# Bank order at three stage changes, and a block's sums of exponentials ahead of the maxima of its slot

## The chip, the core and the metric

The kernel runs on one core of a Trainium2 chip. A core has TensorE (PE), VectorE (DVE), ScalarE (ACT), GpSimd (POOL) and SyncE (SP, which here only issues DMAs); they run their own instruction streams and wait for each other by semaphores. PSUM, where PE writes, has 8 banks of 2 KB for each of 128 partitions; PE, DVE and ACT reach it. The metric is the device time of one execution in microseconds (us): the median of the runs is compared, and one execution more was taken with the hardware profiler.

## The reference, cut to what matters

One step of a trunk of two layers on 128 context tokens and 1024 latent tokens, 1024 wide. Layer 0 has neighbourhood attention beside a state-space mixer, layer 1 grouped-query attention; each layer ends with a gated convolutional feed-forward net (2816 wide).

```python
def odd_mixer(h, od, ctx):              # 16 query heads, 4 key/value heads of 64
    hp = h @ w_in
    q, k, v = ...
    q = rope_2d(rmsnorm(q, q_g)); k = rope_2d(rmsnorm(k, k_g))
    o = blocked_attention(q, jnp.concatenate([k, k_ctx], axis=1), jnp.concatenate([v, v_ctx], axis=1))
    return o.reshape(B, L, GQA_HEADS * HEAD_DIM) @ w_out, None
...
s = jnp.einsum('bqkgd,btkd->bkgqt', qi, k) * scale
p = jax.nn.softmax(s, axis=-1)
o = jnp.einsum('bkgqt,btkd->bqkgd', p, v)
...
x = x + g1 * out                        # output projection, residual
x = x + g2 * conv_ffn(h, w_up, conv_w, conv_b, w_down)
```

## The kernel before

All large products are done in two parts: a weight or an activation is split into a high part (`w_hi`, `mixh`, a copy on ACT that rounds) and a low one (`w_lo`, `mixl`, a subtraction on POOL or DVE), and PE adds three products, hi x hi, hi x lo, lo x hi. Every weight tile so passes SP (load of `w_raw`), ACT (L888) and POOL (L74) before PE has it. There are 4 buffers of `w_raw` and 3 each of `w_hi` and `w_lo`.

**PSUM by stages.** Pools of banks are opened and closed as the stages change. Odd projection: psN1 (2 banks), then psP (3) and psW (3). Grouped attention: psM1 (4), psS1 (2), psO1 (2). Second output projection and feed-forward net: psN2 (1), psD (7). A new pool takes the banks in the order in which it is opened, so that order decides which bank waits for whose last reader.

**Grouped attention (`Grouped.run`, with `finish`, `maxima`, `queries`, `rest`).** t = 0 to 7 goes over pairs of query heads, c = 0, 1 over halves of 512 queries, kt = 0 to 8 over blocks of 128 keys; s = 9c + kt is the slot. In a slot PE makes two score tiles (`gq_ps`, L68) in psS, ACT takes the exponentials (L834), PE adds the slot before to `gq_po` with v (L818, psO), and POOL sums the exponentials into `gq_acc` (DVE at kt = 1). In the same slots PE prepares the maxima for t + 1: matmuls into banks of psM (L735, four in a slot, two in slots 4, 6, 9 and 12, the last by slot 14), each followed by a reduction on DVE (`gq_mx`, L737). psM has four banks in rotation, called `gq_m`; the matmuls that use them take them in the order of issue.

`finish` is a generator that brings the block before to its end while the next one runs. `run` calls `next(done)` once in each slot from kt = 2:

- kt = 2: the sums over keys, called pd: four matmuls of `gq_acc` with ones into a bank of psM (L764); ACT copies two rows out of it (`gq_dn`, L773); SP reshapes them by a load (`gq_d`).
- kt = 4: DVE takes the reciprocals (L780); SP stores them (`d_dn`) and loads them back spread over the partitions (`gq_rd`).
- kt = 7: DVE multiplies, `mix <- gq_po, gq_rd`.

In block (7, 1) the reciprocals (L768) are taken directly from pd's bank, in four pieces. In slot 6 the queries of t + 2 are loaded (`gq_q`, two loads of 576 KB), as soon as their buffer is free, on the same queue of SP as the loads above.

**Order.** In `run` the order of PE and DVE is as written (`manual_schedule`); ACT, POOL and SP, and all engines in the other stages, are ordered by a scheduler from what it takes for the durations, so an edit can move instructions in stages that it doesn't touch.

**Second output projection (`out_proj`).** `mix` is split into `mixh` and `mixl` in four chunks of tokens; then for c = 0, 1, for m = 0 to 7 (128 output features), for h = 0, 1 one accumulation of 24 matmuls (`ps_b`, 128 x 288), added to the residual x by DVE. The function serves both layers.

**Last down projection (L1366).** PE multiplies `ff_f`, which comes back from memory (`ff_r`), with weight tiles loaded one after the other on SP; the residual x is loaded there too.

Of the kernel before, what the change touches and what calls it, by code (L numbers as in the profile page):

```python
# [10 lines left out]
F32 = mybir.dt.float32  # L11
# [3 lines left out]
ALU = mybir.AluOpType  # L15
# [5 lines left out]
KT = 8  # L21
# [623 lines left out]
class Grouped:  # L645
# [104 lines left out]
    def run(self, mix, psM, psS, psO):  # L750
        K, S = self.K, self.S
# [7 lines left out]
        def finish(t, c, po, acc):  # L759

            qs = slice(512 * c, 512 * c + 512)
            pd = bank()
            for p in range(2):
                pe.matmul(pd[64 * p : 64 * p + 64], lhsT=K.ones[:, 0:64], rhs=acc[:, p], start=True, stop=True)  # L764
            rd = tp.tile([128, 512], F32, tag="rd", name="gq_rd", bufs=1)
            if (t, c) == (7, 1):
                for i in range(0, 512, 128):
                    dve.reciprocal(rd[:, i : i + 128], pd[:, i : i + 128])  # L768
                    K.tt(mix[:, t, qs][:, i : i + 128], po[:, i : i + 128], rd[:, i : i + 128], ALU.mult)
                return  # L770
            dn = tp.tile([65, 512], F32, tag="dn", name="gq_dn", bufs=1)
            for p in (0, 64):
                act.activation(dn[p : p + 1], pd[p : p + 1], AF.Copy)  # L773
            d8 = tp.tile([128, 8], F32, tag="d8", name="gq_d8", bufs=1)
            for p in range(2):
                K.load(d8[64 * p : 64 * p + 64], dn[64 * p : 64 * p + 1].rearrange("p (a b) -> p a b", b=8))
            yield
            yield
            r8 = tp.tile([128, 8], F32, tag="r8", name="gq_r8", bufs=1)
            dve.reciprocal(r8, d8)  # L780
            sd = S.dn[(2 * t + c) % 2]
            K.load(sd.rearrange("p (a b) -> (p a) b", b=8), r8)
            for p in range(2):
                K.load(rd[64 * p : 64 * p + 64], bass.AP(tensor=sd.tensor, offset=sd.offset + 512 * p, ap=[[0, 64], [1, 512]]))
            yield
            yield
            yield
            K.tt(mix[:, t, qs], po, rd, ALU.mult)
            yield
# [3 lines left out]
        with K.tc.manual_schedule(engines={mybir.EngineType.PE, mybir.EngineType.DVE}):  # L793
            for t in range(8):
                kv = t // 2
                kk, k2, qq, q2 = self.kk[kv], self.k2[kv], self.qq[t], self.q2[t]
                ahead = self.maxima(t + 1, tp, bank) if t < 7 else iter(())
                keys = self.keys(kv + 1) if t % 2 == 0 and t < 6 else iter(())
                leading = iter(())
                rest = self.rest(t + 1) if t < 7 else iter(())  # L800
                prompt = prompt_attention(
                    K,
                    tp,
                    bank,
                    bank,
                    [(self.qp[t][:, p], self.kp[kv], vt[:, 8, 64 * kv : 64 * kv + 64]) for p in range(2)],
                    mix[:, t, NL:],
                )
                for c in range(2):
                    qs = slice(512 * c, 512 * c + 512)  # L810
                    po = psO.tile([128, 512], F32, tag="o", name="gq_po")
                    acc = ep.tile([128, 2, 512], F32, tag="a", name="gq_acc")
                    pts = {}

                    def value(kt, pts=pts, po=po, acc=acc, kv=kv, t=t):
                        v = vt[:, kt if kt < 8 else 9, 64 * kv : 64 * kv + 64]
                        for p in range(2):
                            pe.matmul(po[64 * p : 64 * p + 64], lhsT=v, rhs=pts[kt][p], start=kt == 0, stop=kt == 8)  # L818
                        for p in range(2):
                            eng = dve if (p == 0 if t == 7 else kt == 1) else pool  # L820
                            if kt == 1:
                                K.tt(acc[:, p], pts[0][p], pts[1][p], ALU.add, eng)
                            elif kt > 1:
                                K.tt(acc[:, p], acc[:, p], pts[kt][p], ALU.add, eng)

                    for kt in range(9):
                        s = 9 * c + kt
                        ks = slice(128 * kt, 128 * kt + 128)
                        pts[kt] = []
                        for p in range(2):  # L830
                            ps = psS.tile([128, 512], F32, tag="s", name="gq_ps")
                            K.acc(ps, [(kk[:, ks], qq[:, p, qs]), (k2[:, ks], q2[:, p, qs])])
                            e = ep.tile([128, 512], F32, tag="p", name="gq_p", bufs=8)
                            act.activation(e, ps, AF.Exp, scale=0.125)  # L834
                            pts[kt].append(e)
                        if 1 <= s <= 5:
                            next(rest, None)
                        if s >= 5:
                            next(keys, None)
                        if s == 6 and t < 6:  # L840
                            self.queries(t + 2)
                            leading = self.leading(t + 2)
                        if s >= 13:
                            next(leading, None)
                        if s in (4, 6, 9, 12):
                            next(prompt, None)
                        while pend:
                            pend.pop(0)()
                        pend.append(lambda kt=kt, value=value: value(kt))
                        for _ in range(1 if s in (4, 6, 9, 12) else 2):  # L850
                            next(ahead, None)
                        if s == 15 and t < 7:
                            self.largest(t + 1)
                        if kt >= 2:
                            next(done, None)
                    for _ in done:
                        pass
                    done = finish(t, c, po, acc)
            while pend:
                pend.pop(0)()  # L860
            for _ in done:
                pass
# [520 lines left out]
def tile_hybrid_step(ctx, tc, I, O):  # L1383
# [204 lines left out]
    def out_proj(l, w, mp, mix, space, source):  # L1588
# [12 lines left out]
        gate = ada[l][:, 16:24]  # L1601
        feed = Feed(K, I, S, l, W, x, rs, A[l][1], ada[l][:, 24:32])
        beside = iter(())
        for c in range(2):
            for m in range(KT):
                cols = lambda ap: ap.rearrange("p (h c t) -> p c h t", h=2, c=2)[:, c]
                u = W.get(w[m])
                K.load(x[c][:, m], cols(source(m)))
                if c and m == KT - 1:
                    feed.tile(0)  # L1610
                for h in range(2):
                    a, b = QCH[2 * h + c]
                    ps = P("b")[:, :HW]
                    K.acc(ps, pairs(u, M(a, b), KT, colm))
                    for s0, s1, cd in segs(a, b):
                        xs = x[c][:, m, h, s0 - a : s1 - a]
                        K.stt(xs, ps[:, s0 - a : s1 - a], gate[:, m, cd : cd + 1], xs, ALU.mult, ALU.add)
                    at = (2 * c + h) * HW
                    norm.add(at, at + HW, x[c][:, m, h], m == KT - 1)
                    if m == KT - 1:  # L1620
                        with K.tc.high_priority():
                            norm.stats(at, at + HW, P)
                    for _ in range(2):
                        next(beside, None)
                    if c and m == KT - 1 and h == 0:
                        feed.ahead(1)
                K.load(cols(S.xs[:, m]), x[c][:, m])
            if c == 0:
                early.release()
                mp.release()  # L1630
                beside = feed.early()
                for _ in range(2):
                    next(beside)
# [87 lines left out]
                normed(u, q, m, a, b)  # L1721
    for p in (tp, norm, x_pool, PB):
        p.release()
    PB = K.psum("psP", b=3)
    psW = K.ps("psW")
    gq = Grouped(K, I, S)
    rp = K.sb("proj1o", 1, "right")
    for m, u, q in first[:2]:
# [31 lines left out]
    for p in (rp, np_, qp):  # L1760
        p.release()
    hp.release()
    psW.release()
    PB.release()
    PN.release()
    mp = K.sb("mix1")
    mix = mp.tile([128, 8, NT], F32, name="mix")
    psM, psS, psO = K.ps("psM1", 4), K.ps("psS1", 2), K.ps("psO1", 2)
    gq.room()
    gq.run(mix, psM, psS, psO)  # L1770
    for p in (psO, psS, psM):
        p.release()
    PN = K.psum("psN2", n=1)
    PB = K.psum("psD", b=7)
# [141 lines left out]
```

## Time and profile before

| | |
|---|---|
| median of 3 runs | 3207.27 us (3204.74 to 3210.99) |
| the profiled execution's own time | 3196.94 us |
| its span | 3195.1 us |
| mean granted clock of PE | 0.967 |
| busy: PE, DVE, ACT, POOL | 2958.6, 1845.8, 1401.5, 1100.6 us |
| grouped attention in the span | about 1840 to 2264 us |
| second output projection | about 2264 to 2379 us |
| last down projection | from about 2907 us to the end |

A row of the timeline gives the start, the duration, the engine, the line of the kernel, the operation with its output and inputs, the number of instructions, and in brackets the idle time before it with what ended that. The granted clock (PEclk) is 1.00 at 2.4 GHz and 0.50 at 1.2 GHz; a window with 0.66 had both.

### The profile page before, as it was taken

What the parts mean: (1) busy time and instruction counts of PE and PEld (TensorE: products, weight loads), DVE (VectorE), ACT (ScalarE), POOL (GpSimd) and SP (SyncE); (2) the same over time, 40 slices, a digit from 0 to 9 for tenths busy, and PEclk for the clock granted to TensorE, in tenths of its full rate; (3) what the DMA queues carried; (4) which work ended last, traced back from release to release, by engine and by line L of the source; (5) the groups of instructions that cost most, each with busy time, mean ns of one, the idle gap of its engine ahead of it and who ended that gap; (6) DMA issues with size and microseconds to landing.
All of it is one profiled execution on the core that took longest, in us unless ns stands there. A gap on an engine that the chain in (4) does not pass through costs nothing.

```text
span 3195.1 us, 49924 instructions
## 1 busy us (share of the span) xinstructions
PE 2958.6 (93%) x19218; PEld 2577.1 (81%) x19218; DVE 1845.8 (58%) x3570; ACT 1401.5 (44%) x2627; POOL 1100.6 (34%) x765
## 2 busy tenths in 40 slices
PE   4998869998999999899998999999888999999999
PEld 3996667797899999788888943434688999998999
DVE  8867856648665555342165666665486565654330
ACT  4335356646444444343253254445454434443332
POOL 1210221153111111355554466667631111113654
PEclk7999989999999999999999999999999999999999
DMA  6657573142212222776634411110331212126653
GB/s 231 167 188 230 172 171 66 32 139 74 69 63 83 75 71 83 255 256 223 227 112 122 119 44 43 26 41 11 122 97 49 83 63 83 63 83 212 209 190 106
DMA packets 207038, 379.56 MB, mean 119 GB/s; under 512 B 36304, under 2 KB 121552, under 8 KB 206672
## 3 DMA queue, kind: packets, MB, share of 16 engines
q1 hardware_dynamic: 206544, 376.31, 37.6%
q8 instruction: 151, 2.47, 0.3%
q14 instruction: 87, 0.71, 0.1%
q0 software_dynamic: 256, 0.07, 0.0%
HBM read 295.80 MB, written 75.13 MB: 116 GB/s over the span
## 4 chain that ended last, share of the span: by engine, by line
PE 46%; DVE 7%; DMA 3%; ACT 1%; issue 1%; SPq 0%; POOL 0%; DVEq 0%; ACTq 0%; POOLq 0%
PE ps_d L1366 16%; PE ps_u L1147 8%; PE ps_b L68 5%; PE ps_w L1147 4%; PE gq_ps L68 3%; PE gq_po L818 3%; PE ps_v L1147 2%; DVE gq_mx L737 2%; DMA w_raw<-in_w_down_dram 1%; DMA d_dn<-gq_r 1%; PE gq_m L735 1%; PE ps_n L933 1%; PE gq_m L764 1%; DVE x L74 1%; DMA gq_rd<-d_dn 1%
## 5 line engine op out<-in xcount | busy, mean ns | idle before, releaser
L74 POOL TENSOR_TENSOR w_lo<-w_raw,w_hi 128x1024 fp32r<-128x1024 f32 x194 | 484.0, 2498 | 579.3 <-ACT w_hi L888 550.7
L1366 PE MATMUL ps_d<-ff_f,w_hi 128*128 128x384 f32 x2112 | 551.8, 340 | 19.8 <-ACT w_hi L888 10.6
L1147 PE MATMUL ps_u<-q_T,ff_w 128*128 128x288 f32 x3168 | 448.3, 297 | 21.9 <-ACT ff_p L1161 15.9
L1147 PEld LDWEIGHTS ps_u<-q_T,ff_w 128*128 128x128 f32 x3168 | 432.0, 189 | 25.1 <-ACT ff_p L1161 17.7
L74 POOL TENSOR_TENSOR ff_w<-w_raw,ff_w 128x512 fp32r<-128x512 f32 x88 | 130.4, 1483 | 882.6 <-ACT ff_w L1135 882.6
L1366 PEld LDWEIGHTS ps_d<-ff_f,w_hi 128*128 128x128 f32 x2112 | 386.2, 190 | 47.6 <-issue 19.5
L1366 PE MATMUL ps_d<-ff_f,w_lo 128*128 128x384 f32 x1056 | 357.2, 338 | 1.5 <-POOL w_lo L74 1.5
L888 ACT ACTIVATE w_hi<-w_raw 128x1024 fp32r<-128x1024 f32 x194 | 204.5, 1055 | 326.3 <-PE ps_d L1366 157.1
L74 POOL TENSOR_TENSOR gq_acc<-gq_acc,gq_p 128x512 f32<-128x512 f32 x210 | 275.1, 1339 | 135.5 <-DVE gq_acc L74 94.4
L71 DVE SCALAR_TENSOR_TENSOR ff_g<-ff_G,pack,ff_g 128x127 f32<-128x127 f32 (+2 forms) x264 | 167.3, 647 | 197.6 <-ACT ff_g L1184 192.9
L1135 ACT ACTIVATE ff_w<-w_raw 128x512 fp32r<-128x512 f32 x266 | 165.4, 624 | 199.6 <-DVE w_raw L74 199.4
L834 ACT ACTIVATE gq_p<-gq_ps 128x512 f32<-128x512 f32 x288 | 158.0, 595 | 147.6 <-PE gq_ps L68 141.8
L737 DVE TENSOR_REDUCE gq_mx<-gq_m 128x1 f32<-128x384 f32 x336 | 164.5, 547 | 96.6 <-PE gq_m L735 96.6
L1366 PEld LDWEIGHTS ps_d<-ff_f,w_lo 128*128 128x128 f32 x1056 | 200.9, 190 | 6.6 <-issue 4.3
L74 DVE TENSOR_TENSOR ff_f<-ff_r,ff_f 128x384 fp32r<-128x384 f32 x130 | 132.7, 1039 | 119.9 <-ACT ff_f L1339 119.9
L71 DVE SCALAR_TENSOR_TENSOR x<-ps_d,ada,x 128x384 f32<-128x384 f32 (+1 forms) x64 | 28.8, 509 | 274.3 <-PE ps_d L1366 274.3
L68 PE MATMUL ps_b<-mixh,w_hi 128*128 128x288 f32 x512 | 152.4, 299 | 11.5 <-DVE gq_rd L768 8.8
L74 DVE TENSOR_TENSOR ff_w<-w_raw,ff_w 128x512 fp32r<-128x512 f32 x178 | 124.6, 701 | 64.4 <-ACT ff_w L1135 64.4
L1147 PE MATMUL ps_v<-q_B,ff_w 128*128 128x288 f32 x1056 | 153.8, 301 | 4.7 <-ACT ff_w L1135 3.0
L1147 PE MATMUL ps_w<-q_B,ff_w 128*128 128x288 f32 x1056 | 150.5, 298 | 8.1 <-ACT ff_p L1168 8.1
L818 PE MATMUL gq_po<-gq_p,gq_v 128*64 128x512 f32 x576 | 157.4, 626 | 0.0
L1147 PEld LDWEIGHTS ps_v<-q_B,ff_w 128*128 128x128 f32 x1056 | 147.9, 193 | 6.0 <-ACT ff_w L1135 3.5
(394 smaller groups left out, 6534.8 us busy)
## 6 DMA issues: line engine op xcount, KB each, us to landing
w_raw<-in_w_down_dram SPq DMA_DIRECT2D x132, 512.0 KB, 4.3
w_raw<-in_w_up_dram SPq DMA_DIRECT2D x88, 512.0 KB, 3.9
w_raw<-in_ada_w_dram SPq DMA_DIRECT2D x80, 512.0 KB, 5.4
d_f<-ff_g SPq DMA_DIRECT2D x44, 576.0 KB, 4.2
ff_r<-d_f SPq DMA_DIRECT2D x130, 192.0 KB, 3.8
w_raw<-in_w_out_dram SPq DMA_DIRECT2D x32, 512.0 KB, 3.7
w_raw<-in_w_qk_dram SPq DMA_DIRECT2D x18, 512.0 KB, 3.8
d_xs<-x SPq DMA_DIRECT2D x32, 288.0 KB, 2.2
```

The costliest lines, as they stand in the source:

```text
L68: self.pe.matmul(ps, lhsT=l, rhs=r, start=i == 0, stop=i == n - 1)
L71: self.dve.scalar_tensor_tensor(out=out, in0=in0, scalar=scalar, in1=in1, op0=op0, op1=op1)
L74: (eng or self.dve).tensor_tensor(out=out, in0=a, in1=b, op=op)
L735: K.pe.matmul(ps[p], lhsT=self.qq[t][h, p, 128 * i : 128 * i + 128], rhs=keys[h, 384 * c : 384 * c + 384], start=True, stop=True)
L737: K.dve.tensor_reduce(out=mx[:, 8 * p + i, c : c + 1], in_=ps[p], axis=AX.X, op=ALU.max)
L764: pe.matmul(pd[64 * p : 64 * p + 64], lhsT=K.ones[:, 0:64], rhs=acc[:, p], start=True, stop=True)
L818: pe.matmul(po[64 * p : 64 * p + 64], lhsT=v, rhs=pts[kt][p], start=kt == 0, stop=kt == 8)
L834: act.activation(e, ps, AF.Exp, scale=0.125)
L888: K.act.activation(hi, raw, AF.Copy)
L1135: K.act.activation(t[:, 0], src, AF.Copy)
L1147: self.K.pe.matmul(ps, lhsT=t[:, p, w], rhs=B(q, k), start=start and k == i == 0, stop=k == 3 and i == 2, skip_group_check=not start)
L1366: K.pe.matmul(ps[j], lhsT=wt[:, w], rhs=ft, start=f == 0 and q == 0, stop=f == NF - 1 and q == 2)
```

## The change

It has four parts. psW is opened before psP for the odd projection, and psS before psM for grouped attention (with the order of release turned to match). In block (7, 1) pd takes a bank of psO. In `run`, `next(done)` moves ahead of the maxima of its slot. In `out_proj` the accumulations of the first half are written as one list, with (m, h) in the order (0, 0), (1, 0), (0, 1), (1, 1) and then as before.

```diff
-            pd = bank()
+            pd = bank() if (t, c) != (7, 1) else psO.tile([128, 512], F32, tag="o", name="gq_po")
...
                         pend.append(lambda kt=kt, value=value: value(kt))
+                        if kt >= 2:
+                            next(done, None)
                         for _ in range(1 if s in (4, 6, 9, 12) else 2):
                             next(ahead, None)
                         if s == 15 and t < 7:
                             self.largest(t + 1)
-                        if kt >= 2:
-                            next(done, None)
...
+            order = [(m, h) for m in range(KT) for h in range(2)]
+            if c == 0:
+                order[1:3] = order[2:0:-1]
+            for m, h in order:
+                if h == 0:
+                    us[m] = W.get(w[m])
+                    K.load(x[c][:, m], cols(source(m)))
...
+                a, b = QCH[2 * h + c]
+                ps = P("b")[:, :HW]
+                K.acc(ps, pairs(us[m], M(a, b), KT, colm))
...
+    psW = K.ps("psW")
     PB = K.psum("psP", b=3)
-    psW = K.ps("psW")
...
-    psM, psS, psO = K.ps("psM1", 4), K.ps("psS1", 2), K.ps("psO1", 2)
+    psS, psM, psO = K.ps("psS1", 2), K.ps("psM1", 4), K.ps("psO1", 2)
```

PE, in one of the 13 blocks that have maxima in slot kt = 2 (`gq_m` are psM's banks):

```order
 L818 MATMUL gq_po<-gq_p,gq_v 64x512 x2
+L764 MATMUL gq_m<-gq_acc,ones 64x512 x2
 L735 MATMUL gq_m<-gq_k_17356,gq_qq 128x384
 L735 MATMUL gq_m<-gq_kk,gq_qq 128x384
 L735 MATMUL gq_m<-gq_k_17356,gq_qq 128x384
 L735 MATMUL gq_m<-gq_kk,gq_qq 128x384
-L764 MATMUL gq_m<-gq_acc,ones 64x512 x2
 L68 MATMUL gq_ps<-gq_qq,gq_kk 128x512
```

pd (L764) moves from behind the slot's four maxima to ahead of them.

DVE, in the first half of a t (`pa` is the small attention over the context tokens, `acc` the two additions of kt = 1):

```order
 L626 RECIPROCAL pa_19027<-pa_19026 128x2
 L74 TENSOR_TENSOR pa_p<-pa_p,pa_19027 128x256
+L737 TENSOR_REDUCE gq_mx<-gq_m 128x1 x2
+L74 TENSOR_TENSOR mix<-gq_po,gq_rd 128x512
+L737 TENSOR_REDUCE gq_mx<-gq_m 128x1 x14
+L74 TENSOR_TENSOR gq_acc<-gq_p 128x512 x2
 L737 TENSOR_REDUCE gq_mx<-gq_m 128x1 x6
-L74 TENSOR_TENSOR mix<-gq_po,gq_rd 128x512
-L737 TENSOR_REDUCE gq_mx<-gq_m 128x1 x10
-L74 TENSOR_TENSOR gq_acc<-gq_p 128x512 x2
```

The multiplication had six reductions between it and `pa_p`, the last four of them slot 7's; now it has two, and slot 7's four come behind it.

SP, last down projection, around the three loads of x (`x<-d_xs`); `w_raw` are weight tiles, `ff_r` the activations. Before:

```order
L63 DMA w_raw<-in_w_down_dram 128x2x512
L63 DMA ff_r<-d_f_94 128x384
L63 DMA ff_r<-d_f_95 128x384
L63 DMA ff_r<-d_f_96 128x384
L63 DMA x_28840<-d_xs 128x8x384
L63 DMA x_28841<-d_xs 128x8x384
L63 DMA x_28842<-d_xs 128x8x384
L63 DMA w_raw<-in_w_down_dram 128x2x512 x7
L63 DMA out_yT_dram<-x_28840 128x384 x4
L63 DMA w_raw<-in_w_down_dram 128x2x512
L63 DMA ff_r<-d_f_97 128x384
```

With the change:

```order
L63 DMA w_raw<-in_w_down_dram 128x2x512
L63 DMA ff_r<-d_f_96 128x384
L63 DMA x_28840<-d_xs 128x8x384
L63 DMA x_28841<-d_xs 128x8x384
L63 DMA x_28842<-d_xs 128x8x384
L63 DMA w_raw<-in_w_down_dram 128x2x512 x5
L63 DMA out_yT_dram<-x_28840 128x384 x2
L63 DMA w_raw<-in_w_down_dram 128x2x512
L63 DMA out_yT_dram<-x_28840 128x384 x2
L63 DMA w_raw<-in_w_down_dram 128x2x512
L63 DMA ff_r<-d_f_97 128x384
```

Between x and `ff_r<-d_f_97` eight loads of `w_raw` stood, and now there are seven: one has moved ahead of x.

## Rows read from the trace of the kernel before

**Rows 1.** the page's first part, busy time of PE, share of the span, instructions

```profile
PE 2958.6 (93%) x19218; PEld 2577.1 (81%) x19218; DVE 1845.8 (58%) x3570; ACT 1401.5 (44%) x2627; POOL 1100.6 (34%) x765
```

**Rows 2.** timeline (start, duration, what, [idle before <- releaser]), PE, odd projection

```profile
1710.17 0.69 PE L68 MATMUL ps_b<-hh,w_hi 128*128 128x384 f32 x1 [7.01 <-DVE q L71]
```

**Rows 3.** timeline at the start of grouped attention, PE and ACT

```profile
1840.48 0.50 PE L68 MATMUL gq_ps<-gq_qq,gq_kk 128*128 128x512 f32 x1 [1.35 <-ACT gq_v L1753]
...
1842.52 1.28 ACT L834 ACT_TABLE_LOAD   x1
```

**Rows 4.** the pd line L764, what its engine waited for (us, times)

```profile
  DVE gq_mx L737: 18.7, 13
```

**Rows 5.** timeline of PE around pd, and of ACT behind it

```profile
1880.87 1.23 PE L764 MATMUL gq_m<-gq_acc,ones 128*64 128x512 f32 x4 [1.95 <-DVE gq_mx L737]
...
1908.59 1.08 PE L764 MATMUL gq_m<-gq_acc,ones 128*64 128x512 f32 x4 [1.52 <-DVE gq_mx L737]
...
1936.47 1.08 PE L764 MATMUL gq_m<-gq_acc,ones 128*64 128x512 f32 x4 [0.94 <-DVE gq_mx L737]
...
1909.71 1.20 ACT L773 ACTIVATE gq_dn<-gq_m 1x512 f32<-1x512 f32 x2 [3.50 <-PE gq_m L764]
```

**Rows 6.** windows: length, busy of PE PEld DVE ACT POOL, PEclk, DMA, GB/s

```profile
1880.00:1890.00 10.00, 9.13 (x28) 3.96 (x30) 3.14 (x7) 4.26 (x8) 6.11 (x5) 0.66 0.15 35
1907.00:1917.00 10.00, 8.48 (x38) 3.85 (x38) 8.58 (x17) 4.37 (x11) 8.13 (x6) 1.00 0.09 12
2097.00:2107.00 10.00, 8.06 (x33) 3.25 (x30) 5.28 (x11) 3.66 (x8) 5.43 (x5) 0.83 0.01 0
2262.00:2282.00 20.00, 11.15 (x60) 9.34 (x58) 17.63 (x25) 10.89 (x33) 16.35 (x17) 0.74 0.73 237
2951.00:2961.00 10.00, 6.14 (x24) 5.04 (x23) 0.00 (x0) 3.18 (x3) 5.70 (x3) 0.83 0.66 243
```

**Rows 7.** timeline of DVE around the multiplication, t = 1, 5, 6

```profile
1923.27 1.95 DVE L737 TENSOR_REDUCE gq_mx<-gq_m 128x1 f32<-128x384 f32 x4 [0.85 <-PE gq_m L735]
1927.13 0.69 DVE L74 TENSOR_TENSOR mix<-gq_po,gq_rd 128x512 f32<-128x512 f32 x1 [1.91 <-DMA gq_rd<-d_dn]
1927.74 1.94 DVE L737 TENSOR_REDUCE gq_mx<-gq_m 128x1 f32<-128x384 f32 x4
...
2145.30 0.69 DVE L74 TENSOR_TENSOR mix<-gq_po,gq_rd 128x512 f32<-128x512 f32 x1 [2.35 <-DMA gq_rd<-d_dn]
...
2195.91 0.68 DVE L74 TENSOR_TENSOR mix<-gq_po,gq_rd 128x512 f32<-128x512 f32 x1
```

**Rows 8.** DMA issues of 1914 to 1925: count, size, us to landing

```profile
gq_q<-d_qd SPq DMA_DIRECT2D x2, 576.0 KB, 6.5
d_dn<-gq_r SPq DMA_DIRECT2D x1, 4.0 KB, 6.2
```

**Rows 9.** timeline of PE, maxima of slots 7 and 8 at t = 1

```profile
1922.79 0.44 PE L735 MATMUL gq_m<-gq_k,gq_qq 64*128 64x384 f32 x1
...
1925.47 0.44 PE L735 MATMUL gq_m<-gq_k,gq_qq 64*128 64x384 f32 x1
...
1925.75 0.34 PE L735 MATMUL gq_m<-gq_k,gq_qq 64*128 64x384 f32 x1
```

**Rows 10.** second output projection: timeline of PE, DVE, POOL; the chain of waits

```profile
2273.39 0.58 PE L68 MATMUL ps_b<-mixh,w_hi 128*128 128x288 f32 x1 [8.85 <-DVE gq_rd L768]
...
2269.53 2.66 DVE L74 TENSOR_TENSOR mixl<-mix,mixh 128x288 fp32r<-128x288 f32 x3
...
2265.49 6.38 POOL L74 TENSOR_TENSOR mixl<-mix,mixh 128x288 fp32r<-128x288 f32 x7 [2.07 <-ACT mixh L1599]
...
2273.39 54.51 PE ps_b L68 x393
```

**Rows 11.** last down projection: timeline of SP and PE

```profile
2935.76 4.47 SPq L63 DMA_DIRECT2D x<-d_xs  x3
...
2955.27 0.97 PE L1366 MATMUL ps_d<-ff_f,w_hi 128*128 128x384 f32 x4 [3.47 <-ACT w_hi L888]
```

More of the change, by code (lines that the diff above doesn't have):

```diff
@@ L1603, in out_proj @@
         beside = iter(())
+        us = {}
         for c in range(2):
[L1605 to L1627, printed above, removed]
@@ new lines, in out_proj @@
+            cols = lambda ap: ap.rearrange("p (h c t) -> p c h t", h=2, c=2)[:, c]
+            order = [(m, h) for m in range(KT) for h in range(2)]
[5 more added lines that the diff above has]
+                    K.load(x[c][:, m], cols(source(m)))
+                    if c and m == KT - 1:
+                        feed.tile(0)
+                a, b = QCH[2 * h + c]
+                ps = P("b")[:, :HW]
+                K.acc(ps, pairs(us[m], M(a, b), KT, colm))
+                for s0, s1, cd in segs(a, b):
+                    xs = x[c][:, m, h, s0 - a : s1 - a]
+                    K.stt(xs, ps[:, s0 - a : s1 - a], gate[:, m, cd : cd + 1], xs, ALU.mult, ALU.add)
+                at = (2 * c + h) * HW
+                norm.add(at, at + HW, x[c][:, m, h], m == KT - 1)
+                if m == KT - 1:
+                    with K.tc.high_priority():
+                        norm.stats(at, at + HW, P)
+                for _ in range(2):
+                    next(beside, None)
+                if c and m == KT - 1 and h == 0:
+                    feed.ahead(1)
+                if h:
+                    K.load(cols(S.xs[:, m]), x[c][:, m])
@@ L1762, in tile_hybrid_step @@
     hp.release()
+    PB.release()
     psW.release()
-    PB.release()
     PN.release()
@@ L1767, in tile_hybrid_step @@
     mix = mp.tile([128, 8, NT], F32, name="mix")
-    psM, psS, psO = K.ps("psM1", 4), K.ps("psS1", 2), K.ps("psO1", 2)
+    psS, psM, psO = K.ps("psS1", 2), K.ps("psM1", 4), K.ps("psO1", 2)
     gq.room()
     gq.run(mix, psM, psS, psO)
-    for p in (psO, psS, psM):
+    for p in (psO, psM, psS):
         p.release()
```

## The prediction

> **What bounds the kernel now.** The page comes first: PE is busy for 2958.6 us, 93% of the span [rows 1]. The remaining 7% is idle PE, some 236 us, so a change that only moves work can pay where it takes idle time, or half clock, from PE, and can lose by adding either. The next view is the timeline of PE around every place that the diff touches, with what ended each wait; then DVE, ACT and SP at the same moments; last the windows, for the granted clock. Five places come out of that, and each is costed alone. The sum is made against the profiled execution, 3196.94 us, which lies 10.3 us under the median of the runs, 3207.27; I add the sum to the median.
>
> **1. Banks at the odd projection (psW before psP).** The long wait there is 7.01 us for DVE's q [rows 2]: the fourth accumulation in a pool of three banks waits for the eviction of the first of its turn, and that is the same turn on whichever banks the pool lies. The order of DVE and SP stays. Cost 0; no other wait over 1 us in that start ends at a bank.
>
> **2. Banks at the start of grouped attention (psS before psM).** PE's first scores wait 1.35 us for the last eviction of v [rows 3] and would now start that much earlier. But the exponentials behind them wait for ACT, which still has its copies and a table load of 1.28 us at 1842.52 to run first [rows 3]; the score pool has two banks, so PE would only reach the next wait sooner. I take 0; the ends are 0 and the 1.35 us gained.
>
> **3. The sums of exponentials (pd) before the maxima, 13 blocks.** Two matmuls per half, called pd, follow the maxima and wait for their bank: 18.7 us in 13 waits, all ended by DVE's reductions [rows 4]. There are three kinds: 1.95 us (3 times), 1.52 to 1.54 (6) and 0.92 to 0.94 (4) [rows 5]. Ahead of the maxima pd takes a bank that was reduced a slot ago, and does not wait. But now the slot's last maximum gets pd's bank and waits for ACT's two copies out of it: pd ends at 1908.59 + 1.08 = 1909.67, the copies at 1909.71 + 1.20 = 1910.91 [rows 5], 1.24 us later. Beside this PE runs the pair before it, which takes 0.28 (1925.47 to 1925.75) [rows 9]. So about 1.0 us of new wait replaces the old one: 3 x 0.95 + 6 x 0.5 - 4 x 0.05 = **5.7 us gained**. The ends are 18.7 (no new wait) and 18.7 - 13 x 1.24 = 2.6.
>
> **4. The clock behind the three long waits.** Right after each 1.95-us wait the granted clock falls to half: 0.66 over ten us in two such windows (one of them shown), 0.83 in the third, against 1.00 around a wait of 1.52 [rows 6]. That is 3.4 + 3.4 + 1.7 = 8.5 us of full speed; PE is busy some 0.9 of it, so 7.7 us. The new waits of 1.0 us are of the size that left the clock at 2.4 GHz, so I count **7.7 us gained**; the ends are 0 and 8.5.
>
> **5. The multiplication by the reciprocals, moved ahead of four reductions.** The same line of the diff moves the block's later steps. In kt = 7 of the first half of t = 1 to 5, DVE now runs mix<-gq_po,gq_rd before the reductions of that slot, not after them. That step waits for a DMA: 1.91 us at t = 1, 2.35 at t = 5, and at each t between [rows 7]. It is late because d_dn (4 KB, 6.2 us to landing) goes out behind the 1152 KB of gq_q, and only then can gq_rd be loaded [rows 8]. That queue keeps its order, and its starting point moves with the slots, so the multiplication still starts when it does now. What is queued behind it now matters. Before: slot 7's four reductions end at 1923.27 + 1.95, so slot 8's maxima have their banks at 1925.47; only slot 8's own reductions stand behind the multiplication (1927.74) [rows 7, 9]. After: slot 7's stand there, and slot 8's maxima start when the first of them ends, 1927.13 + 0.69 + 0.49 = 1928.3. PE stands 2.8 us, then goes at DVE's pace. All behind the multiplication is later by one slot of maxima, 1925.47 - 1922.79 = 2.68 us [rows 9]; what PE now waits in slot 9 is already in that difference. Five times: **13.4 us lost**. At t = 6 no gq_q is loaded and the step waits for nothing (2195.91) [rows 7], so nothing is lost there, nor in second halves, where no reductions stand behind it. The ends are 0 (the data come before slot 7) and 20, if nothing of slot 9's present wait is won back: slot 8's last maxima would then be done with at 1927.13 + 0.69 + 1.94 = 1929.76, not 1925.75, five times 4.0.
> The Trainium skill (DMA: Bandwidth & Descriptors, Rules for kernel authors) advises to wait on a transfer's semaphore late; this move waits earlier, and the waits ended by gq_rd agree with it.
>
> **6. The clock behind these new waits.** No row shows a PE wait of 2.8 us here. The nearest rows are on either side: 1.95 us, followed each time by half clock, and 8.85 us at the end of the stage [rows 10], with 0.74 over 20 us, 5.2 us lost [rows 6]. Below is 0, if they pass as the 1.5-us waits do. I take the nearer: 7.7 / 3 = 2.6 each, four times of five, **10 us lost** (ends 0 and 26).
>
> **7. Start of the second output projection.** PE stands 8.85 us until 2273.39, for the reciprocals that read pd's bank [rows 10]: the first accumulation has that bank. With pd in psO and psM elsewhere it has a free one. Then mixl sets the pace: POOL's run of seven starts at 2265.49 and lasts 6.38, its four of the first chunk thus to about 2269; DVE's last of that chunk is the first of the three from 2269.53 [rows 10], done near 2270.4. So the first accumulation ends at about 2271 and the second, of the same chunk by the new order, follows; before, nothing had been done at 2273.39. Both run partly at half clock, before and after. Two accumulations are 48 matmuls of 0.14 us (54.51 / 393 in the chain of waits [rows 10], a part of it at half clock), 6.7 us at the start's own pace; against it stands that the second begins with the clock still down, some 1 us: **5.8 us gained**, ends 0 and 8.85. It is kept, since the normalisation behind it starts when PE ends the first half. The same swap of order in layer 0 changes nothing, since its first accumulation needs the same late tile first.
>
> **8. Start of the last down projection.** Nothing there is edited, but ACT's and SP's order moves: one more load of w_raw stands ahead of the three 1.6-MB loads of x. Now PE waits 3.47 us for w_hi, whose load was queued behind x from 2935.76 on [rows 11], and the window shows 0.83, 1.7 us [rows 6]. One weight tile more in hand covers about 4 us of PE: **4.5 us gained**, ends 0 and 5.2.
>
> **Sum.** - 5.7 - 7.7 + 13.4 + 10 - 5.8 - 4.5 = -0.3: 3196.6 for the profiled execution, **3207** for the median. About 0.2%, 6.4 us, is what a measurement of this kernel can tell from no change: 3200.9 to 3213.7 counts as the same.
>
> **Rivals.**
> A. The clock stays up behind the multiplication's waits, or falls once only: its price shrinks from 10 to 0 to 3, and the sum is -7 to -10: 3198, faster. For it: ten waits up to 1.54 left the clock at 1.00. Against it: all three of 1.95 did not. It decides at the granted clock in the ten us after each of the five waits.
> B. Slower: behind these waits the clock stays down longer than behind 1.95 us, since they are longer. At 4 us each, between 2.6 and the 5.2 of the 8.85-us wait, five cost 20 in place of 10: +10, 3217. It decides at 0.6 or less over ten us. By the Trainium skill (TensorE: Matmul & The Clock Gate, A second HAM failure mode: psum-queue depth-cycling), short idling between groups that cycle through banks is enough to make the clock swing; the ten short waits here do not agree, the three long ones do.
> C. gq_rd comes in time for slot 7, so the move costs nothing: 5.7 + 7.7 + 5.8 + 4.5 = 23.7 gained, 3184. Against it is the fixed order of the queue.
> D. The two starts (7, 8) give nothing, because mixl and x arrive no sooner: -0.3 + 10.3 = +10, 3217.
>
> **Chances.** Forecast 0.40, A 0.30, B 0.18, C 0.05, D 0.07. Of the forecast 0.04 falls to each side of the bound; of A 0.02 and of B and D 0.03 fall back within it. Faster 0.30 - 0.02 + 0.05 + 0.04 = 0.37, slower 0.25 - 0.03 + 0.04 = 0.26, same 0.37. The range takes in A and B with the ends of the small terms: 3194 to 3219. The likeliest case alone has 3201 to 3213.
>
> **What would show it.** In the changed profile: the waits of pd for gq_mx gone, with about 1 us before a fourth maximum ended by gq_dn; the clock at 1.00 near 1885 and 1994; a PE wait of 2.6 to 3.7 us at L735 five times, ended by DVE, right behind mix<-gq_po,gq_rd, and half clock after it; the 8.85 us cut to short waits on mixl; the 3.47 us gone. I am wrong if those five waits are absent or under 1.5 us, or if they are there and the clock stays at 2.4 GHz.

## The result, and the profile after

The changed kernel takes 3222.20 us (median of 5 runs, 3216.46 to 3226.93), the kernel before beside it 3207.07 (3201.65 to 3210.99); the ratio is 1.0058, 95% interval 1.0039 to 1.0076. It is slower by some 15 to 19 us where 0 was forecast, and 3 us above the range. The profiled execution took 3226.93 us, 30 more than that of before. About 9 of these 30 lie ahead of the grouped attention, 6.9 of them before the odd projection even begins, where, but for one swap of order in layer 0, the work is the same; among the variants below the start of grouped attention lies anywhere from 1840 to 1853 us. The profile of before lay 10 us under its median, this one 5 above its own. So stages are compared, each from its own start (a slot is counted from its first scores to the first scores of the next):

| stage (us, from PE's rows) | before | after | |
|---|---|---|---|
| grouped attention, first scores to the end of t = 6 | 380.5 | 401.3 | +20.8 |
| of it slots 8 to 10 of t = 1 to 5 | 48.1 | 77.9 | +29.8 |
| of it slots 2, 5, 6 and 11 to 13, all t | | | -10.5 |
| of it the rest, nearly all in the first slot of t = 0 | | | +1.5 |
| t = 7 to the end of the output projection | 157.5 | 155.8 | -1.7 |
| last down projection | 283.2 | 285.3 | +2.1 |

The loss is in three slots of five blocks. The first view is PE's timeline there: the first maxima of slot 8 at t = 1 to 5, with the wait before each in brackets. None of the kernel before's matmuls at this line waited at all.

```profile
1934.47 0.44 PE L735 MATMUL gq_m<-gq_k,gq_qq 64*128 64x384 f32 x1 [2.84 <-DVE gq_mx L737]
...
1992.15 0.44 PE L735 MATMUL gq_m<-gq_k,gq_qq 64*128 64x384 f32 x1 [1.77 <-DVE gq_mx L737]
...
2053.88 0.44 PE L735 MATMUL gq_m<-gq_k,gq_qq 64*128 64x384 f32 x1 [3.46 <-DVE gq_mx L737]
...
2112.25 0.43 PE L735 MATMUL gq_m<-gq_k,gq_qq 64*128 64x384 f32 x1 [2.79 <-DVE gq_mx L737]
...
2172.02 0.68 PE L735 MATMUL gq_m<-gq_k,gq_qq 64*128 64x384 f32 x1 [3.18 <-DVE gq_mx L737]
```

The releaser named is a reduction on DVE. DVE's timeline at t = 1 says why it was late, and the DMA view of 1920 to 1934 (count, size, median us from issue to landing) says what DVE stood for:

```profile
1927.01 1.01 DVE L737 TENSOR_REDUCE gq_mx<-gq_m 128x1 f32<-128x384 f32 x2
1933.26 0.69 DVE L74 TENSOR_TENSOR mix<-gq_po,gq_rd 128x512 f32<-128x512 f32 x1 [5.25 <-DMA gq_rd<-d_dn]
1933.87 3.33 DVE L737 TENSOR_REDUCE gq_mx<-gq_m 128x1 f32<-128x384 f32 x7
```

```profile
gq_q<-d_qd SPq DMA_DIRECT2D x2, 576.0 KB, 6.3
...
d_dn<-gq_r SPq DMA_DIRECT2D x1, 4.0 KB, 6.9
```

DVE idles 5.25 us with slot 7's four reductions queued behind the multiplication, where before it had run them first and idled 1.91 [rows 7]. The 4 KB are still behind 1152 KB of queries [rows 8]. Then seven reductions run in one go.

The windows of ten us behind the five waits (length, busy PE, PEld, DVE, ACT, POOL, granted clock, DMA, GB/s) give the rest of the loss; the first row, around pd of t = 0, shows what was gained:

```profile
1886.00:1896.00 10.00, 9.22 (x44) 4.09 (x42) 7.20 (x15) 4.81 (x11) 5.64 (x5) 1.00 0.15 35
1934.00:1944.00 10.00, 9.46 (x24) 4.29 (x24) 4.69 (x10) 2.55 (x5) 0.37 (x1) 0.66 0.00 0
1993.00:2003.00 10.00, 9.95 (x25) 4.16 (x24) 3.65 (x9) 3.15 (x7) 0.28 (x1) 0.54 0.01 2
2054.00:2064.00 10.00, 9.93 (x28) 4.50 (x28) 4.11 (x10) 2.58 (x5) 0.00 (x0) 0.66 0.00 0
2113.00:2123.00 10.00, 9.97 (x23) 4.19 (x22) 3.75 (x9) 3.15 (x7) 0.00 (x0) 0.51 0.00 0
2172.00:2182.00 10.00, 9.98 (x31) 4.99 (x32) 4.99 (x11) 2.55 (x5) 0.00 (x0) 0.70 0.01 2
```

PE is full in the five lower rows and does half the work for most of each: 0.66 over ten us is 6.8 us at 1.2 GHz. By the clock records of the trace the five stretches last 6.8, 13.7, 6.8, 10.2 and 6.8 us; 40.7 us of them lie in slots 8 to 10, which costs 20.4 us of the 29.8. The other 9.4 is what PE stands still longer than before (its idle time in these slots, read by itself, goes from 4.3 to 14.3). In the first row the clock is at 1.00, where it was 0.66 [rows 6].

The last two places are the ends of banks and weights. PE at the start of the output projection, and the DVE row that it waits for:

```profile
2294.64 0.40 PE L68 MATMUL ps_b<-mixh,w_hi 128*128 128x288 f32 x1 [0.53 <-ACT mixh L1599]
2295.47 0.40 PE L68 MATMUL ps_b<-mixl,w_hi 128*128 128x288 f32 x1 [0.43 <-DVE mixl L74]
2297.20 0.40 PE L68 MATMUL ps_b<-mixl,w_hi 128*128 128x288 f32 x1 [0.42 <-DVE mixl L74]
2304.99 0.58 PE L68 MATMUL ps_b<-mixh,w_hi 128*128 128x288 f32 x1 [3.68 <-DVE mix L74]
```

```profile
2304.57 0.28 DVE L74 TENSOR_TENSOR mix<-gq_po,gq_rd 128x128 f32<-128x128 f32 x1
```

The wait of 8.85 us [rows 10] is gone from the first accumulation, and 3.68 has appeared before the second: that one's bank is `gq_po`, which DVE's last multiplication still reads.

SP and PE in the last down projection, which begins at 2935.5 (before at 2907.7):

```profile
2966.14 1.46 SPq L63 DMA_DIRECT2D w_raw<-in_w_down_dram  x1
2967.69 0.42 SPq L63 DMA_DIRECT2D ff_r<-d_f  x1
2968.16 5.71 SPq L63 DMA_DIRECT2D x<-d_xs  x3
```

```profile
2964.90 0.44 PE L1366 MATMUL ps_d<-ff_f,w_lo 128*128 128x384 f32 x1 [1.98 <-POOL w_lo L74]
2969.78 0.44 PE L1366 MATMUL ps_d<-ff_f,w_lo 128*128 128x384 f32 x1 [0.44 <-POOL w_lo L74]
...
2988.49 0.79 PE L1366 MATMUL ps_d<-ff_f,w_hi 128*128 128x384 f32 x3 [1.94 <-ACT w_hi L888]
2990.93 0.69 PE L1366 MATMUL ps_d<-ff_f,w_lo 128*128 128x384 f32 x1 [1.65 <-POOL w_lo L74]
```

The weight tile ahead of x makes x leave 32.7 us after the stage's start, not 28.1 [rows 11], so the tiles behind x come later by about as much as PE has one more in hand. One wait of 3.47 and one of 0.39 have become four, 6.0 in all.

### The profile page after: what moved, and what is told of

It reads as the page before. It is cut to its first block, busy times and chain, and to the rows that moved or that the text cites. A ratio compares the mean times of both kernels' runs of the same rounds, so it can differ in the third digit from the quotient of the medians.

```text
span 3225.0 us, 49933 instructions
## 1 busy us (share of the span) xinstructions
PE 2982.5 (92%) x19218; PEld 2590.2 (80%) x19218; DVE 1855.9 (58%) x3570; ACT 1400.5 (43%) x2627; POOL 1092.2 (34%) x765
## 5 line engine op out<-in xcount | busy, mean ns | idle before, releaser
L74 POOL TENSOR_TENSOR w_lo<-w_raw,w_hi 128x1024 fp32r<-128x1024 f32 x194 | 473.7, 2445 | 579.8 <-ACT w_hi L888 526.4
L74 DVE TENSOR_TENSOR ff_f<-ff_r,ff_f 128x384 fp32r<-128x384 f32 x130 | 139.3, 1089 | 127.3 <-ACT ff_f L1339 125.9
L68 PE MATMUL ps_b<-mixl,w_hi 128*128 128x288 f32 x512 | 152.6, 298 | 0.9 <-DVE mixl L74 0.9
```

What stands on the lines that cost most here:

```text
L68: self.pe.matmul(ps, lhsT=l, rhs=r, start=i == 0, stop=i == n - 1)
L74: (eng or self.dve).tensor_tensor(out=out, in0=a, in1=b, op=op)
```

## The experiments

Each variant was timed in five rounds beside the kernel before; ratios are to that. "Slots 8 to 10" are the five values of t = 1 to 5; 9.1 to 10.2 us in the kernel before, 14.7 to 16.6 in the changed one.

**1. Which edit costs (e1, e2).** e1 is the kernel before with only this:

```diff
+                        if kt >= 2:
+                            next(done, None)
                         for _ in range(1 if s in (4, 6, 9, 12) else 2):
                             next(ahead, None)
...
-                        if kt >= 2:
-                            next(done, None)
```

> The kernel before with one edit: next(done) ahead of the maxima, nothing else of the change. Theory (the multiplication that now stands ahead of four reductions waits for gq_rd, and half clock follows): grouped attention is 21 us longer, as in the profile of the change, so about 3228 us. Rival 1 (the banks, or the order that the scheduler made of the other stages, cost the time): 3207 us, no change.

e2 is the changed kernel with the same lines put back.

> The changed kernel with next(done) put back behind the maxima; banks, psO for the last pd and the order of the output projection stay. Theory: the loss is gone, 3205 us, since the output projection gives some 2 us and the down projection has its old order. Rival 1: 3222 us, as the changed kernel.

e1: 3217.45 us against 3200.74, ratio 1.0053 (1.0036 to 1.0069), some 17 us where 21 were expected; slots 8 to 10 take 14.5 to 15.6. e2: 3200.30, 0.9995 (0.9981 to 1.001). So the loss comes with the move of `next(done)`, and the bank and order edits together are worth nothing that can be measured. e1's windows behind its waits all read alike:

```profile
1933.00:1943.00 10.00, 9.97 (x30) 4.86 (x30) 4.31 (x10) 2.55 (x5) 0.00 (x0) 0.66 0.00 0
...
2165.00:2175.00 10.00, 9.98 (x30) 4.71 (x31) 4.55 (x10) 2.55 (x5) 0.00 (x0) 0.66 0.01 2
```

**2. Which step of it (e3, e9).** e3 moves kt = 2 (pd) alone ahead, e9 all but kt = 7 (the multiplication). Against the changed kernel e9 is this; e3 has `kt == 2` and `kt > 2` in its place.

```diff
-                        if kt >= 2:
+                        if kt >= 2 and kt != 7:
                             next(done, None)
...
+                        if kt == 7:
+                            next(done, None)
```

> The changed kernel with only the first of the three steps (kt = 2, pd) ahead of the maxima; the reciprocals and the multiplication behind them as before. Theory: 12 to 13 us under e2, 3192 us: 5.7 us of bank waits and 7.7 us of half clock at the three long ones are gone. Rival 2 (pd ahead of the maxima is itself what costs, by the wait of the fourth maximum for the copies out of its bank): 3210 us or more.

> The changed kernel, with the step of kt = 7 (the multiplication) alone put back behind the maxima of its slot; the sums (kt = 2) and the reciprocals (kt = 4) stay ahead. Theory: the whole loss comes from the place of the multiplication on DVE. Then the five waits of PE at L735 in slot 8 are gone, slots 8 to 10 of t = 1 to 5 take 9 to 10.2 us as in the kernel before (15 to 16.6 in the changed one), and the time is that of the kernel with the sums alone ahead, ratio 0.997 to 1.000 to the kernel before. Rival 1: the loss comes from the bank rotation that pd's move shifts, wherever the multiplication stands: slots 8 to 10 stay at 14 us or more and the ratio is 1.004 to 1.006. Rival 2: the earlier reciprocals bring gq_rd earlier and are worth something of their own: the ratio is 0.996 or less.

e3: 3197.52 us, 0.9991 (0.9975 to 1.0008). e9: 3199.64 against 3202.27, 0.999 (0.9971 to 1.0008). With the multiplication behind its slot's reductions the loss is gone, though the banks rotate as in the changed kernel; so it is the multiplication's place. The summary of line L735, what PE waited for there (us, times), first the changed kernel, then e9:

```profile
  DVE gq_mx L737: 16.9, 12
  ACT gq_dn L773: 7.0, 9
```

```profile
  ACT gq_dn L773: 7.0, 9
  DVE gq_mx L737: 2.9, 7
```

Two parts of the expectations failed. e3 was expected 12 to 13 us under e2, at 3192; it is 3 us under it, and the intervals overlap. And slots 8 to 10 of e9 are 11.3, 9.2, 12.1, 9.4 and 15.0, not 9 to 10.2: the multiplication still waits for gq_rd, now with only slot 8's reductions behind it, and PE meets that in slot 9. In both variants this is worst at t = 5 (3.13 us in e9), here in e3, with the window behind it:

```profile
2137.53 0.69 PE L631 MATMUL gq_m<-pack,pa_p 128*128 128x128 f32 x2 [2.72 <-DVE gq_mx L737]
```

```profile
2137.00:2147.00 10.00, 9.47 (x24) 3.87 (x24) 4.59 (x11) 1.75 (x4) 0.00 (x0) 0.52 0.00 0
```

**3. Are the data the cause (e4, e5, e7).** The multiplication waits because d_dn and gq_rd stand behind gq_q on SP. e4 is the changed kernel with SP's order in `run` as written, which puts gq_q behind them:

```diff
-        with K.tc.manual_schedule(engines={mybir.EngineType.PE, mybir.EngineType.DVE}):
+        with K.tc.manual_schedule(engines={mybir.EngineType.PE, mybir.EngineType.DVE, mybir.EngineType.SP}):
```

> The changed kernel with SP's order in grouped attention as written, so that d_dn and gq_rd go out ahead of the 1152 KB of gq_q; the multiplication keeps its place ahead of the reductions. Theory: gq_rd lands before slot 7, the five waits and the half clock behind them are gone, slots 8 to 10 take 8.1 us as at t = 6 in place of 15.6: 3222 - 37 = 3185 us. Rival 3 (the multiplication costs by its place on DVE, whatever it waits for): 3215 us or more.

3198.87 us, 0.9996 (0.998 to 1.0012). The DMA view of 1925 to 1940 has the 4 KB:

```profile
d_dn<-gq_r SPq DMA_DIRECT2D x1, 4.0 KB, 1.4
```

They land in 1.4 us, not 6.9, and slots 8 to 10 fall to 8.1 to 8.8, under the kernel before: the multiplication costs by its place only while its data are late. But the time is only that of the kernel before, where 3185 was expected, since SP's order moved another load. At t = 2 and 4 the next keys, gq_k, now stand behind gq_rd, DVE waits for them in slot 6, and PE behind it for 4.99 and 4.76 us, each time with 6.8 us of half clock. PE, DVE and SP at t = 2:

```profile
1988.70 0.68 PE L735 MATMUL gq_m<-gq_k,gq_qq 64*128 64x384 f32 x1 [4.99 <-DVE gq_mx L737]
```

```profile
1987.49 0.68 DVE L74 TENSOR_TENSOR gq_kk<-gq_k,gq_k 64x512 fp32r<-64x512 f32 x1 [6.46 <-ACT gq_k L673]
```

```profile
1981.65 1.10 SPq L63 DMA_DIRECT2D gq_rd<-d_dn  x2
1982.79 0.59 SPq L63 DMA_DIRECT2D gq_k<-d_kd  x1
```

e5 loads these keys at the start of t as well:

```diff
         K.load(k[:, NT:], self.I["cgk"][64 * kv : 64 * kv + 64])
+        if kv:
+            yield
...
                 keys = self.keys(kv + 1) if t % 2 == 0 and t < 6 else iter(())
+                next(keys, None)
```

> The changed kernel with SP's order as written (as e4) and the loads of the next keys issued at the start of t, so that nothing on SP stands between them and their use. Theory: all five slots 8 to 10 take 8.1 us, no wait at t = 2 and 4 either, no half clock from t = 1 on: 18 us under e4, 20 us under the kernel before, ratio 0.994. Rival (e4's new waits at t = 2 and 4 come from gq_q itself, which now starts later): ratio 0.999 or 1.000, as e4.

3192.97 us against 3201.59, 0.9969 (0.9953 to 0.9985): the loss has become a gain, though a smaller one than 0.994. Slots 8 to 10 take the 8.1 us expected at t = 1, 3 and 5, but 11.4 and 9.8 at t = 2 and 4: there PE still waits 0.44 and 0.43 us for a reduction in slot 8, and at t = 2 the clock is at half for 3.4 us soon after. e7 has e5's edits of the loads (SP's order and the early keys) in the kernel before, and nothing of the change:

> The kernel before, nothing of the change, with SP's order as written and the keys' loads at the start of t. It prices what the late gq_rd cost the kernel before and, against e5, what the change is worth when the data are in time. Theory: the waits of slot 9 (1.3, 0.3, 1.0, 0.9, 1.8 us) go, 5 us less than before, ratio 0.998, and e5 is some 12 us under this kernel. Rival: the change is worth nothing even with the data in time, e5 and this one agree within 3 us.

3194.84 us, 0.9979 (0.9965 to 0.9993). So most of e5's gain is that of the loads; by the medians the change itself was worth 2 us there, not the 12 expected, and the intervals overlap, so the rival that it is worth nothing is not excluded.

**4. How much is the clock (e6).** e6 is the changed kernel with twelve matmuls that nobody reads, put on PE before slot 8's maxima of t = 1 to 5, where it stood still:

```diff
+                        if s == 8 and 1 <= t <= 5:
+                            warm = psS.tile([128, 512], F32, tag="s", name="gq_ps")
+                            for _ in range(6):
+                                K.acc(warm, [(kk[:, ks], qq[:, 0, qs]), (k2[:, ks], q2[:, 0, qs])])
```

> The changed kernel with twelve more matmuls (six products of the score kind, whose result nobody reads) on PE ahead of the maxima of slot 8 for t = 1 to 5: they fill the 2.8 us in which PE waits for DVE and end when the wait does. Theory (more than half of the loss is half clock behind an idle PE): the clock stays up, slots 8 to 10 take 11 us in place of 15.6, ratio to before 1.000. Rival (the wait alone costs it, the clock is a sign only): ratio 1.005 as the changed kernel, or more with the added work.

3209.94 us, 1.0016 (1.0002 to 1.003). More work makes the changed kernel faster: by the two ratios, whose intervals do not meet, 0.4%, some two thirds of the loss. In the traces slots 8 to 10 fall from 77.9 to 68.1 us in all. The filler takes about as long as the waits that it fills (twelve of some 0.235 us are 2.8 us; the five waits are 2.8 in the mean), so what it gives back is the clock. Behind the filler it stays up at t = 2, 3 and 4, and these slots take 11.4 to 12.9 us, near the 11 expected; at t = 5 it falls for 3.4 us (14.6). At t = 1 (17.0) it falls for 13.7 us all the same, behind ten us in which PE was busy for 9.73; this window, the one after it, and the one behind the filler at t = 2:

```profile
1926.00:1936.00 10.00, 9.73 (x37) 5.10 (x36) 4.42 (x10) 2.17 (x4) 7.00 (x6) 0.95 0.20 49
1935.00:1945.00 10.00, 10.00 (x26) 4.19 (x25) 2.84 (x7) 2.66 (x5) 0.00 (x0) 0.50 0.00 0
1994.00:2004.00 10.00, 10.00 (x45) 4.96 (x45) 7.42 (x16) 4.01 (x9) 1.32 (x2) 1.00 0.00 0
```

**5. The bank of gq_po, and a version that beats both (e8, e10, e11).** e8 is e5 with the pools of grouped attention opened in a third order (and released in the order that matches):

```diff
-    psS, psM, psO = K.ps("psS1", 2), K.ps("psM1", 4), K.ps("psO1", 2)
+    psS, psO, psM = K.ps("psS1", 2), K.ps("psO1", 2), K.ps("psM1", 4)
```

> e5 with the pools of grouped attention opened in the order psS, psO, psM, so that the second, third and fourth accumulation of the output projection get banks of psM, free for long, and not the two of psO, which DVE's last multiplication reads until 10 us into the stage. Theory (the bank of gq_po held the second accumulation in the changed kernel): the wait of 3.7 to 4.1 us is gone, some 4 us under e5. Rival (mixl sets the pace anyway): the wait moves to mixl, 0 to 1 us.

3187.09 us, 0.9943 (0.9921 to 0.9965): faster than the kernel before and than the changed one, and 6 us under e5, where 4 were expected. PE's waits at the start of its output projection are these three, and there is none before the second accumulation:

```profile
2261.31 0.40 PE L68 MATMUL ps_b<-mixh,w_hi 128*128 128x288 f32 x1 [0.53 <-ACT mixh L1602]
2262.14 0.40 PE L68 MATMUL ps_b<-mixl,w_hi 128*128 128x288 f32 x1 [0.43 <-DVE mixl L74]
2263.88 0.40 PE L68 MATMUL ps_b<-mixl,w_hi 128*128 128x288 f32 x1 [0.42 <-DVE mixl L74]
```

From t = 7 to the end of the projection it takes 150.6 us, against 157.2 in e5 and 157.5 in the kernel before. Against e5 that is the wait of 3.74 us before the second accumulation, and half clock, 10.2 us of it in e5's stretch and 3.4 in e8's.

Last, e10 is e8 once more, and e11 the same with `next(done)` put back behind the maxima (e10's label says otherwise; its text says what it is).

> The fastest variant so far once more (changed kernel, loads of SP in written order, keys a t earlier, pools opened psS, psO, psM), so that it stands beside its twin of this job on the same chip. Expected: ratio 0.992 to 0.9965 to the kernel before, gq_po's bank no longer waited for in the second accumulation of the output projection.

> The same variant with next(done) put back behind the maxima of its slot. It asks what the move of next(done) is worth when the multiplication's data are in time. Theory: the waits of pd for gq_mx (0.9 to 1.95 us, 13 times) and the dips behind the long ones come back and nothing else, so it is 4 to 10 us slower than the variant of this job with next(done) ahead. Rival: the move is worth nothing, because the fourth maximum's wait for gq_dn (0.78 us) and the longer slots 5 and 6 take back what pd's waits gave, and the clock falls about as often: the two agree within 3 us.

e10: 3185.23 us against 3202.27, 0.9948 (0.9929 to 0.9967). e11: 3190.31, 0.9966 (0.9952 to 0.998). By the medians the move is worth 5 us when its data are in time, as the theory had it, and in the traces grouped attention to the end of t = 6 takes 367.0 and 375.4 us; but the intervals overlap, so a gain is likely and not shown. In e11 pd's waits are back; the summary of pd's line has the same numbers as [rows 4]:

```profile
  DVE gq_mx L739: 18.7, 13
```

## Why the prediction was wrong, step by step

The mechanism was there: five waits of 1.8 to 3.5 us at L735, ended by DVE, right behind the multiplication, with half clock after each. What turned no change into a loss is the size of step 6, and two gains that did not come. Against the forecast of -0.3 the traces give +21.2 from the first scores of grouped attention on; the medians give 15 to 19, so a few of the 21 belong to these two executions.

**Steps 1 and 2** (0): right. The odd projection's long wait is 6.99 us, as before. The first scores do come earlier, 4.85 us ahead of the first exponential and not 3.34, and PE only reaches the next wait sooner, as step 2 said: this is the table's +1.5, counted from the earlier start, and no loss.

**Steps 3 and 4** (-13.4): right in kind, -10.5. All 13 waits of pd are gone, and the fourth maximum waits 0.78 us nine times for gq_dn (7.0 in all), where 1.0 was forecast, and 0.47 four times for a reduction; the clock stays at 1.00. Not foreseen: slots 5 and 6 are longer, by 0.1 us mostly, by 0.6 at t = 0 and 0.9 at t = 2 and 4, 2.8 us in all. That pd's turn of the four banks does this is likely and was not tested alone.

**Step 5** (+13.4): right in kind, 9.4 over five blocks, and with step 6 it makes the loss, as e1 and e9 show. The waits are 2.8 us in the mean, as forecast, 14.0 in all. But the 4.2 us that PE stood in slot 9 of the kernel before are gone, and step 5 had them down as already counted. Two of these four waits of the kernel before, at t = 1 and 5:

```profile
1928.34 0.44 PE L631 MATMUL gq_m<-pack,pa_p 128*128 128x128 f32 x2 [1.11 <-DVE gq_mx L737]
...
2146.51 0.44 PE L631 MATMUL gq_m<-pack,pa_p 128*128 128x128 f32 x2 [1.55 <-DVE gq_mx L737]
```

**Step 6** (+10): the step that failed most. It took the nearer of two rows, 2.6 us of lost speed behind each 1.95-us wait, four times of five. Measured is 20.4 us in slots 8 to 10, 4.1 each, behind all five, and 1.8 more in the slots behind t = 2's (they are in the -10.5): the clock stays down for 6.8 to 13.7 us. That is the sum of rival B, 4 each and 20 in all, and its 0.18 was too low. But that the mean came to B's 4 is luck, since its reason, that longer waits keep the clock down longer, does not hold. Its sign, 0.6 or less over ten us, shows at t = 2 and 4 alone (0.54 and 0.51), behind the two shortest waits; behind the three longest the clock is down for 6.8 us, no longer than behind two of the 1.95-us waits of the kernel before. Step 6 explains 10 of the 21 us, step 8 some 7 and step 7 some 4; what steps 3 and 4 gave less (3) and step 5 cost less (4) nearly cancel, and 1.5 is the earlier start. e6 shows, at t = 2 to 4, that the clock is a cause of its own, not a sign of waiting. The Trainium skill (TensorE: Matmul & The Clock Gate, A second HAM failure mode: psum-queue depth-cycling) tells of a kernel whose clock swings because PE idles shortly and frequently between matmul groups that cycle through banks. Here it fell behind single waits of 1.8 to 3.5 us, some 60 us apart, five times of five, and the short ones of 0.78 us here and of 1.5 us in the kernel before left the clock at 1.00.

**Step 7** (-5.8): failed; -1.7 by the traces, and the same in e1 (156.0 us for the stretch, against 155.8) without the bank edits. I had looked for the reader of the first accumulation's bank and not of the second's. In the program's addresses the pool behind takes the banks in the order 1, 7, 6, 5, 2, 3, 4, not by their numbers, and in the changed kernel bank 7 holds `gq_po` until DVE's fourth piece is done. Once neither of the first two banks is late, as in e8, the gain is there: 6.9 us against the kernel before. The wait in the first accumulation is gone in e1 too, without the bank edits: there the shifted rotation alone puts the pd of (7, 1) on another bank.

**Step 8** (-4.5): failed; +2.1. I counted the weight tile that comes earlier, and not that its load delays x and all behind x by as much. No run isolated it, and two executions of one kernel (e8 and e10) differ by 2.3 us in this stage. But SP has the new order in e5, e8 and e10 as well: these three and the changed kernel take 283.3 to 285.6 us, 284.8 in the mean, and the nine with the order of before 281.7 to 285.3, 283.0 in the mean. So some 2 us of loss are likely the order's own, and a gain of 4.5 is excluded.

**Rivals.** A fell, since the clock stayed down five times. C did not come by itself. Built on purpose it gave 9 us (e5, but 7 of them without the change, e7) and, with the bank of e8, 14 of the rival's 24. D was nearly right in its number, -1.7 and +2.1 where it had 0; of its reasons, that mixl and x arrive no sooner, the first was wrong, since the bank held step 7. B and D together, which I had treated as alternatives, give 10 + 10 = 20 over the forecast, 3227, against 3222 measured.

What stays open: why e6's clock fell for so long at t = 1 and not at t = 2 to 4, and why the waits are followed now by 6.8 and now by 13.7 us of half clock, the longest stretch behind the shortest wait.

## What to carry to other kernels

In an engine's fixed order, an instruction that waits for a transfer belongs behind everything that others are waiting for; moving it up without moving its data up turned 2 us of idle DVE into a stall of PE. The Trainium skill (DMA: Bandwidth & Descriptors, Rules for kernel authors) says to wait on a transfer late, and e9 agrees with it: that one step put back is worth the whole loss. A stall of PE of 2 to 3 us is to be priced with the slow stretch behind it, here 20 us for waits of 14 in all. When a pool takes over banks, list the last reader of each of the first two or three, not of the first alone.

## What was not expected of the hardware

A wait under one microsecond can be followed by a longer slow stretch than any behind the long waits above. In e2 PE waited 0.91 us at t = 4, and the next twenty us ran at 1.2 GHz, though PE was busy for 18.95 of them; waits of 0.85 to 1.16 us at the same place in three other blocks left the clock alone.

```profile
2097.64 0.69 PE L631 MATMUL gq_m<-pack,pa_p 128*128 128x128 f32 x2 [0.91 <-DVE gq_mx L737]
```

```profile
2097.00:2117.00 20.00, 18.95 (x48) 7.00 (x48) 9.25 (x20) 6.33 (x13) 4.88 (x4) 0.50 0.00 0
```

And unread matmuls in an idle stretch can pay for themselves (e6), which says that here PE's idle time has a price beyond its length.
